# The second copy of K's high and low parts: computed twice, or moved by a DMA inside SBUF

## The chip, the cores and the metric

The kernel runs on one core of one Trainium2 chip. The metric is the device time of one execution in microseconds. A core has TensorE (PE, matrix products, with its weight loads listed apart as PEld), VectorE (DVE), ScalarE (ACT), GpSimd (POOL) and SyncE (SP, which here only issues DMAs), and 16 DMA engines that all queues share.

## The reference

One layer of a decoder trunk on x of 2048 x 1024 floats (one batch entry):

```python
u = x * (1.0 + scale[:, None, :]) + shift[:, None, :]
h = u @ w_in[l]
q, k, v, a_gate, p_in, p_gate, m_a, m_p = jnp.split(h, offsets, axis=-1)
a = sliding_window_sink_attention(q, k, v, sinks[l], bias, mask) * jax.nn.silu(a_gate)
a = a @ w_attn_proj[l]
...                       # a causal pooling branch p, with its own gate and projection
y = jax.nn.sigmoid(m_a) * a + jax.nn.sigmoid(m_p) * p
y = (y @ w_out[l]) * (1.0 + gate[:, None, :])
x = layer_norm(DEEPNORM_ALPHA * x + y, ln_gain[l], ln_bias[l])
```

Attention has 16 query heads of 64 and 2 key/value heads of 64. It goes block by block over 128 positions, and each block of queries sees its own and the preceding block of keys. `shift`, `scale` and `gate` come from a small product with SiLU(c).

## The kernel before, in words

**Two parts of every number.** TensorE is fed with the type float32r. Each operand is split into a high part, a copy into that type by ScalarE (`copy`), and a low part, the difference of the original and the high part, by VectorE (`low`, whose instruction is line 132 of the profile). A product is made as high x high + high x low + low x high (`mm3`): 12 matmuls for a 512 x 512 piece of contraction.

**Fast products.** The large projections are computed with the two-by-two scheme that needs 7 block products where 8 are usual, with 15 sums (Strassen-Winograd). A `Quad` is a pair of output row blocks by two halves of 512 columns. Its moving operands are eight sets in SBUF (`B11`, `T1`, `T2`, `B21`, `T3`, `B22`, `T4`, `B12`), split ahead of time; its weights are loaded raw into `W` and `A22`, summed by GpSimd (lines 294 to 303) and split into `w_set` (lines 325 and 332). `front` makes the first two products of a quad, `back` the other five, and `ring` walks through groups of two quads, two at a time. Between products it calls `tick`, which runs what is hung there: loads, splits, stores.

**Phases.** The sequence is worked in two halves of 1024 positions (s = 0, 1), each as two column halves of 512 (t = 0, 1). The first phase projects K, V and all gates of half 0; then comes attention of half 0 together with its q and pooling projections; then the same two for half 1; then the output projections and the norm. The last ticks of attention of half 0 already compute the first products of the first two quads of half 1. The first of these two is the K/V quad, and the second a gate quad, so K of half 1 is taken as soon as the phase changes.

**The place of the change.** `kv_quad`'s `consume` calls `take_k(s, t, kp)` when the PSUM tile `kp` holds K for 512 positions: rows 0 to 63 are K of kv head 0, rows 64 to 127 of kv head 1. `kk` is an SBUF tile of 128 partitions x (kv head) x (high, low) x (128 + 1024) positions. Attention needs each kv head on both halves of the partitions, since `qs` holds the high part of a query head on one half and its low part on the other. So `take_k` writes each kv head twice: ScalarE copies the high part to the half where it lies (line 697) and VectorE makes the low part (line 132), and then both do it again with the other half as target. This gives 4 copies and 4 differences a call, and 16 of each in all. Line 691 moves the last 128 columns of the first half to the front of the tile for half 1. Attention reads `kk` in `score_mms` (`lg<-kk,qs` in the profile).

**Behind it in `back`.** In a group whose second pair of weights is already split, `back` does for its first quad: add the saved `u` on VectorE (line 380), copy `p5` on ScalarE (line 381, `p<-mm`), form the next sum (line 383), then `consume` (here `take_k`). For its second quad it copies `u2` first (line 376, `u<-mm`), and then lets the product B21 add into the accumulator that was copied.

**What sets the order.** Instructions called through the wrappers `pe`, `act`, `dve`, `pool` and `sp` (line 56) stay in program order on their engine. Those called through `nc.scalar`, `nc.vector`, `nc.gpsimd` and `nc.sync` are placed by a planner that uses its own costs and due times; it also sets all semaphores. `take_k` uses the second kind. TensorE's order is fixed throughout. An engine's queue is worked strictly in order, SP's too: a DMA that waits for its source or for its room holds up those behind it.

Of the kernel before, what the change touches and what calls it, by code (L numbers as in the profile page):

```python
# [23 lines left out]
CH = 512  # L24
# [3 lines left out]
HD = 64  # L28
# [31 lines left out]
def kernel(  # L60
# [22 lines left out]
    nc = tc.nc  # L83
# [44 lines left out]
    def as32(ap):  # L128
        return ap.bitcast(F32)

    def low(engine, dst, src, hi):
        engine.tensor_tensor(dst, src, as32(hi), ALU.subtract)  # L132
# [416 lines left out]
    def kv_quad(s):  # L549
        vts = []  # L550

        def consume(ph, mi, t, src):
            if mi == 0:
                if s == 0 and t == 0:
                    place_kv(ph)
                take_k(s, t, src)
            else:
                vt = ph.c("vt")
                nc.scalar.copy(vt, src)
                vts.append((t, vt))  # L560

        def turn(i):
            if s > 0 and i == 0:
                nc.vector.tensor_copy(vv[:, 0], vv[:, 2 * NB])
            turn_v(*vts[i])

        return Quad((win[TK], win[TV]), consume), turn
# [121 lines left out]
    def take_k(s, t, kp):  # L689
        if s > 0 and t == 0:  # L690
            nc.vector.tensor_copy(kk[:, :, :, 0:P], kk[:, :, :, 2 * CH :])
        c0 = P + t * CH
        for kv in range(2):
            src = kp[kv * HD : kv * HD + HD, :]
            for half in (kv, 1 - kv):
                dst = kk[half * HD : half * HD + HD, kv, :, c0 : c0 + CH]
                nc.scalar.copy(dst[:, 0, :], src)
                low(nc.vector, dst[:, 1, :], src, kk[kv * HD : kv * HD + HD, kv, 0, c0 : c0 + CH])

    def bias_rows():  # L700
        room = cp.tile([P, 4 * D], F32, tag="set_T2", name="head_T2")
# [683 lines left out]
    kk = vv = None  # L1385
# [127 lines left out]
```

## Time and profile before

| | |
|---|---|
| median of 3 runs | 1752.56 us (1752.3 to 1756.21) |
| profiled execution, span from the first to the last instruction | 1751.3 us |
| granted TensorE clock, mean | 0.993 |
| ScalarE K copies (line 697) | 16, mean 582 ns |
| VectorE K differences (line 132, `kk<-mm,kk`) | 16, mean 688 ns |
| K written, half 0 | 384.8 to 400.9 us |
| K written, half 1 | 689.1 to 709.1 us |
| first scores of attention | 417.7 us |

No time of the profiled execution is known besides its span; it is 1.3 us under the median of the runs. In the profile's rows a group reads: line, engine, operation, output<-input by the program's names, shapes, count. A row of the timeline begins with the start and the duration in us and may end with how long the engine had stood idle and which instruction ended that. The rows of a table by stretches give the length of the stretch, the busy time of the engines (with counts), TensorE's granted clock, the DMA engines' share and their GB/s.

### The profile page before, as it was taken

How to read it: one execution, taken by the hardware profiler on the slowest of the kernel's cores; microseconds unless marked ns; L12 is line 12 of the kernel's file. 1: busy time of each engine (PE TensorE's matmuls, PEld its weight loads, DVE VectorE, ACT ScalarE, POOL GpSimd, SP SyncE). 2: the span in 40 equal slices, each digit the busy share in tenths (PEclk: the TensorE clock that was granted, in tenths of full speed). 3: DMA queues.
4: the chain of work that ended last, by engine and by line, in shares of the span. 5: the costliest groups of instructions: out<-in, count | busy, mean ns of one | idle time of the engine just before them, and what ended most of it. 6: DMA issues, size and time to landing. Idle time of an engine off the chain costs nothing.

```text
span 1751.3 us, 24998 instructions
## 1 busy us (share of the span) xinstructions
PE 1697.7 (97%) x8248; PEld 1427.4 (82%) x8248; DVE 1205.2 (69%) x2178; ACT 934.0 (53%) x1973; POOL 798.3 (46%) x618
## 2 busy tenths in 40 slices
PE   6899999999999998999999999999999999999996
PEld 5688888878888887888788888888888878887785
DVE  5977665655777777767645357777768696865777
ACT  4644444545777776545444367777745353423452
POOL 2154444441356567434424124555773572463542
PEclk9999999999999999999999999999999999999999
DMA  9384758743354558687777634544698675699432
GB/s 365 117 283 177 276 204 280 257 155 132 114 169 142 178 187 318 237 284 255 276 265 257 234 111 133 180 140 157 232 351 289 185 265 194 216 341 360 157 139 102
DMA packets 185843, 381.31 MB, mean 218 GB/s; under 512 B 18785, under 2 KB 39281, under 8 KB 185713
## 3 DMA queue, kind: packets, MB, share of 16 engines
q1 hardware_dynamic: 179072, 363.92, 59.7%
q0 software_dynamic: 3552, 11.56, 1.7%
q10 hardware_dynamic: 3088, 4.23, 0.8%
q8 instruction: 65, 1.06, 0.2%
q14 instruction: 66, 0.53, 0.1%
HBM read 244.35 MB, written 138.44 MB: 219 GB/s over the span
## 4 chain that ended last, share of the span: by engine, by line
PE 42%; POOL 3%; DVE 2%; DMA 2%; issue 1%; ACT 1%; POOLq 0%; SPq 0%; DVEq 0%; ACTq 0%
PE mm L56 25%; PE lg L56 14%; PE pv L56 2%; PE pt L56 1%; DMA set_T<-ain_T_split 1%; DVE w_set L132 1%; POOL nxt L56 1%; POOL W L298 0%; DVE wide L56 0%; POOL p L56 0%; POOL wide L601 0%; DMA W<-in_wap_dram 0%; POOL rs L56 0%; ACT L L56 0%; POOL a L56 0%
## 5 line engine op out<-in xcount | busy, mean ns | idle before, releaser
L56 PE MATMUL mm<-set_B,w_set 128*128 128x512 f32 x3240 | 799.0, 395 | 12.6 <-ACT u L376 6.3
L56 PEld LDWEIGHTS mm<-set_B,w_set 128*128 128x128 f32 x3240 | 603.2, 189 | 140.7 <-DVE w_set L132 8.8
L56 PE MATMUL lg<-set_T,w_set 128*128 128x512 f32 x2088 | 504.4, 392 | 11.8 <-DVE w_set L132 5.1
L56 PEld LDWEIGHTS lg<-set_T,w_set 128*128 128x128 f32 x2088 | 391.3, 188 | 99.5 <-DVE w_set L132 8.0
L132 DVE TENSOR_TENSOR w_set<-W,w_set 128x1024 fp32r<-128x1024 f32 x162 | 224.0, 1383 | 182.7 <-ACT w_set L325 172.1
L325 ACT CAST w_set<-W 128x1024 fp32r<-128x1024 f32 x162 | 170.6, 1053 | 291.1 <-PE mm L56 221.6
L56 PE MATMUL mm<-set_T,w_set 128*128 128x512 f32 x1080 | 265.6, 394 | 0.0
L56 PEld LDWEIGHTS mm<-set_T,w_set 128*128 128x128 f32 x1080 | 200.7, 188 | 41.1
L294 POOL TENSOR_TENSOR W<-W,A 128x512 f32<-128x512 f32 x56 | 83.8, 1497 | 218.3 <-DMA W<-in_win_dram 59.4
L303 POOL TENSOR_TENSOR W<-W 128x512 f32<-128x512 f32 x56 | 83.5, 1492 | 165.5 <-DVE w_set L132 150.3
L56 DVE TENSOR_TENSOR o<-pv,o 64x128 f32<-64x128 f32 x256 | 72.4, 283 | 88.6 <-ACT o L56 85.5
L56 ACT ACTIVATE L<-L,nm 128x257 f32<-128x257 f32 (+1 forms) x256 | 127.7, 501 | 9.4 <-DVE nm L56 3.9
L298 POOL TENSOR_TENSOR W<-W 128x512 f32<-128x512 f32 x56 | 90.9, 1624 | 78.6 <-DVE w_set L132 68.9
L56 DVE CUSTOM_DVE_ANT_0 L<-lg,bt,nsink 128x256 f32<-128x256 f32 (+1 forms) x256 | 111.6, 473 | 5.0 <-PE lg L56 0.8
L299 POOL TENSOR_TENSOR W<-W 128x512 f32<-128x512 f32 x56 | 88.6, 1582 | 33.6 <-DMA W<-in_win_dram 26.6
L56 POOL TENSOR_TENSOR w_set<-W,w_set 128x1024 fp32r<-128x1024 f32 x14 | 33.7, 2410 | 139.7 <-ACT w_set L56 97.0
L56 POOL TENSOR_TENSOR p<-nxt,pg 128x512 f32<-128x512 f32 x32 | 41.9, 1311 | 107.0 <-DVE sm L56 104.6
L56 ACT COPY o<-pv 64x256 f32<-64x256 f32 x128 | 47.5, 371 | 76.7 <-PE pv L56 76.0
L56 DVE TENSOR_TENSOR ptl<-pt,pth 128x512 fp32r<-128x512 f32 (+1 forms) x128 | 85.8, 670 | 1.9 <-ACT pth L56 1.7
L56 PE MATMUL lg<-kk,qs 128*128 128x256 f32 (+1 forms) x512 | 80.5, 279 | 0.0
L56 ACT ACTIVATE L<-L,sm 128x256 f32<-128x256 f32 (+1 forms) x128 | 64.5, 504 | 30.0 <-DVE sm L56 30.0
L56 DVE TENSOR_TENSOR k_lo<-spare,k_hi 128x512 fp32r<-128x512 f32 x61 | 60.4, 992 | 28.5 <-ACT k_hi L56 13.4
(216 smaller groups left out, 2308.2 us busy)
## 6 DMA issues: line engine op xcount, KB each, us to landing
W<-in_win_dram SPq DMA_DIRECT2D x48, 512.0 KB, 5.2
w_set<-wmix_d SPq DMA_DIRECT2D x32, 512.0 KB, 5.2
W<-in_win_dram SPq DMA_DIRECT2D x34, 256.0 KB, 3.2
A<-in_win_dram SPq DMA_DIRECT2D x34, 256.0 KB, 5.0
ag_d<-sig SPq DMA_DIRECT2D x32, 256.0 KB, 3.9
pg_d<-sig SPq DMA_DIRECT2D x32, 256.0 KB, 3.8
ma_d<-sig SPq DMA_DIRECT2D x32, 256.0 KB, 3.9
mp_d<-sig SPq DMA_DIRECT2D x32, 256.0 KB, 3.8
```

Source lines behind the costliest of these rows:

```text
L56: return lambda *args, **kw: self.tc.keep_in_program_order(op(*args, **kw))
L132: engine.tensor_tensor(dst, src, as32(hi), ALU.subtract)
L294: e.tensor_tensor(self.w[:, 1, :], self.w[:, 2, :], self.a22, ALU.add)
L298: e.tensor_tensor(x[:, 1, :], x[:, 1, :], x[:, 0, :], ALU.subtract)
L299: e.tensor_tensor(x[:, 2, :], x[:, 0, :], x[:, 2, :], ALU.subtract)
L303: e.tensor_tensor(x[:, 3, :], x[:, 3, :], x[:, 1, :], ALU.subtract)
L325: a.copy(by_two(hi), raw)
```

## The change

For each kv head `take_k` now makes the high and the low part once, on the half of the partitions where K lies. Both are then brought to the other half by one DMA from SBUF to SBUF (64 partitions x 2 x 512 floats, 256 KB), issued by `nc.sync` and placed by the planner. There are two such transfers a call and 8 in the kernel, in place of 8 copies and 8 differences.

```diff
@@ def take_k(s, t, kp)
         for kv in range(2):
             src = kp[kv * HD : kv * HD + HD, :]
-            for half in (kv, 1 - kv):
-                dst = kk[half * HD : half * HD + HD, kv, :, c0 : c0 + CH]
-                nc.scalar.copy(dst[:, 0, :], src)
-                low(nc.vector, dst[:, 1, :], src, kk[kv * HD : kv * HD + HD, kv, 0, c0 : c0 + CH])
+            dst = kk[kv * HD : kv * HD + HD, kv, :, c0 : c0 + CH]
+            nc.scalar.copy(dst[:, 0, :], src)
+            low(nc.vector, dst[:, 1, :], src, dst[:, 0, :])
+            nc.sync.dma_start(as32(kk[(1 - kv) * HD : (2 - kv) * HD, kv, :, c0 : c0 + CH]), as32(dst))
```

## The prediction

> **What bounds the kernel now.** First the page's head, then the list of who waited for whom on the TensorE, then the busy time of three stretches: the end of the first projection phase and the start of attention (372 to 421 us), the stretch in which the second K tile is first written (689 to 696 us), and the rest of the second projection phase.
>
> ```profile
> span 1751.3 us, 24998 instructions
> PE 1697.7 (97%) x8248; PEld 1427.4 (82%) x8248; DVE 1205.2 (69%) x2178; ACT 934.0 (53%) x1973; POOL 798.3 (46%) x618
> PE mm L56 <- ACT u L376: 6.3, 1, 6.3
> 372.00:421.00 49.00, 49.00 (x223) 40.42 (x222) 25.68 (x37) 23.00 (x36) 6.14 (x4) 1.00 0.34 113
> 689.00:696.00 7.00, 0.70 (x3) 0.39 (x2) 4.98 (x9) 3.51 (x7) 5.31 (x5) 0.73 1.02 411
> 696.00:1011.00 315.00, 313.53 (x1380) 258.84 (x1380) 184.60 (x202) 146.59 (x225) 115.55 (x80) 1.00 0.74 260
> ```
>
> TensorE is busy 97% of the span, so work taken from ScalarE or VectorE counts only where TensorE stands still for it. Around the first phase's K writes it does not: 49.00 of 49.00 us are busy. Before the second phase's first K write it does, once, for 6.3 us, and the engine that it waits for is ScalarE, with the copy `u` of line 376. In that stretch the DMA engines are full (share 1.02, 411 GB/s). The timeline of all engines there:
>
> ```profile
> 686.38 1.39 SPq L56 DMA_DIRECT2D set_T<-u_T_split  x3
> 686.40 2.91 PE L56 MATMUL lg<-set_T,w_set 128*128 128x512 f32 x12
> 689.13 0.58 ACT L697 CAST kk<-mm 64x512 fp32r<-64x512 f32 x1
> 690.49 0.68 DVE L132 TENSOR_TENSOR kk<-mm,kk 64x512 fp32r<-64x512 f32 x1
> 690.54 1.26 POOL L56 TENSOR_TENSOR a<-o,ag 128x512 f32<-128x512 f32 x1 [1.66 <-DVE o L56]
> 691.20 0.58 ACT L697 CAST kk<-mm 64x512 fp32r<-64x512 f32 x1 [1.49 <-DVE kk L132]
> 691.82 0.69 DVE L132 TENSOR_TENSOR kk<-mm,kk 64x512 fp32r<-64x512 f32 x1 [0.65 <-ACT kk L697]
> 692.53 0.58 ACT L697 CAST kk<-mm 64x512 fp32r<-64x512 f32 x1 [0.75 <-DVE kk L132]
> 693.88 0.58 ACT L697 CAST kk<-mm 64x512 fp32r<-64x512 f32 x1 [0.76 <-DVE kk L132]
> 694.48 0.59 ACT L381 COPY p<-mm 128x512 f32<-128x512 f32 x1
> 694.97 0.59 ACT L376 COPY u<-mm 128x512 f32<-128x512 f32 x1
> 695.61 10.03 PE L56 MATMUL mm<-set_B,w_set 128*128 128x512 f32 x36 [6.30 <-ACT u L376]
> ```
>
> Four K copies stand on ScalarE ahead of the copies `p` and `u`, and from the second on each waits for the VectorE difference before it. Even the third, which reads the other 64 rows of the same PSUM tile, does so. Copy and difference alternate at about 1.35 us a pair. `u` saves an accumulator that the B21 product then adds into, so TensorE stops from 689.3 to 695.6.
>
> **Part by part.** The K instructions and their users, from the answer on the tile `kk`:
>
> ```profile
> L56 PE MATMUL lg<-kk,qs x512: 220/281/288, 417.7 to 1276.7; 128*128 128x256 f32 x160, 128*128 128x128 f32 x11
> L697 ACT CAST kk<-mm x16: 573/582/586, 384.8 to 707.8; 64x512 fp32r<-64x512 f32 x16
> L132 DVE TENSOR_TENSOR kk<-mm,kk x16: 674/688/695, 386.1 to 708.4; 64x512 fp32r<-64x512 f32 x16
> L691 DVE CAST kk<-kk x1: 428/428/428, 400.9 to 400.9; 128x512 fp32r<-128x512 f32 x1
> busy tenths in 40 slices 0000000013444443100000034444400000000000
> 400.18 0.69 DVE L132 TENSOR_TENSOR kk<-mm,kk 64x512 fp32r<-64x512 f32 x1 [0.65 <-ACT kk L697]
> 413.02 0.76 DVE L132 TENSOR_TENSOR vv<-pt,vv 128x256 fp32r<-128x256 f32 x2 [9.26 <-ACT vv L685]
> ```
>
> *Removed:* 8 ScalarE copies of 0.582 us and 8 VectorE differences of 0.688 us, 4.7 and 5.5 us of engine time. In the first phase that is worth nothing, since TensorE has no gap there to close. In the second, the two pairs at 692.53 and 693.88 go. `p` also has a floor: it fills a tile of the new phase where attention's buffers lay, and the POOL product that read the last of these ends at 690.54 + 1.26 = 691.80. The second copy ends at 691.78, so the floor does not bite. `u` moves from 694.97 to about 692.3 and TensorE restarts near 692.95: **2.65 us** earlier.
>
> *Added:* 8 transfers of 256 KB (64 rows of 2 x 512 floats) on SP's queue, 2 per K write. Their landing is covered in both phases. The first scores of attention start at 417.7, 17.5 us after the last difference at 400.18. In the second phase the line of tenths shows `kk` unused from slice 17 to 22, hundreds of microseconds. The copy of line 691 now has to wait on VectorE for the last two transfers. Behind it are weights and V of the first phase, but VectorE is idle 9.26 us before 413.02, so I cost it at nothing (without that cover, about one landing). On SP the first phase's transfers stand ahead of attention's first weights and the gate stores; TensorE's gapless 49 us say that these come early, so nothing again, and one issue each if they did not.
>
> *What is late next.* SP's queue does not move with TensorE in this place:
>
> ```profile
> SPq L56 <- DMA ain_T<-a: 12.6, 1, 12.6
> ain_T<-a POOLq DMA_DIRECT2D x2, 256.0 KB, 4.7
> ain_B<-a SPq DMA_DIRECT2D x1, 256.0 KB, 2.0
> 703.02 0.34 SPq L56 DMA_DIRECT2D A<-in_win_dram  x1
> 704.02 0.59 SPq L56 DMA_DIRECT2D set_T<-u_T_split  x1
> set_T<-u_T_split SPq DMA_DIRECT2D x1, 1024.0 KB, 7.9
> 705.48 8.32 PE L56 MATMUL lg<-set_T,w_set 128*128 128x512 f32 x36
> 720.24 1.67 DVE L132 TENSOR_TENSOR w_set<-W,w_set 128x1024 fp32r<-128x1024 f32 x1 [0.57 <-ACT w_set L325]
> 722.73 2.88 PE L56 MATMUL mm<-set_B,w_set 128*128 128x512 f32 x12
> ```
>
> SP stands 12.6 us, until 703.02, because room for the next weights is freed by POOL's four stores of attention's last tiles. Those hang on POOL and the DMA engines, not on TensorE. Only then come the weights `A`, `W` and the second half of set T4 at 704.02, which lands 7.9 us later, at 711.9. TensorE needs that half after two T3 products and half of a T4 product, 30 of the 36 matmuls from 705.48: 705.48 + 30 x 8.32/36 = 712.4. The slack is **0.5 us**. A second check is the next pair's weights: the VectorE difference ends at 721.91, TensorE takes it with the third matmul from 722.73, at about 723.2, slack 1.3 us. So of the 2.65 us about 0.5 is kept and the rest is spent waiting for T4.
>
> *What the new transfers cost there.* The first pair is ready at 691.2 and 692.5, when the DMA engines are full: 0.52 MB at 411 GB/s is 1.3 us of their time, ahead of POOL's stores. SP's restart, and with it T4, slips by 0 to 1.3; I take 0.6, the middle, as stores of another queue share the engines with it. The second pair comes when SP issues T4 and the next weights. Two issues of 0.34 to 0.59 us each and again up to 1.3 us of traffic give 0 to 2 us, against slack that is partly there; I take 0.3 on the path. **Sum: -0.5 + 0.6 + 0.3 = +0.4 us**; its ends are -0.5 and 1.3 + 2 - 0.5 = +2.8.
>
> The SBUF page of the Trainium skill ("SBUF — State Buffer", Door 1: The DMA port swizzle) speaks against the change: 64 partitions reach half of the DMA ports and get about half the rate. By it each pair would weigh 2.6 us rather than 1.3 and the sum would be about +1.4 us; no K transfer is in this trace to show it.
>
> *The clock.* The stall also costs TensorE speed. The rows give the length of a stretch, TensorE's busy time in it and the granted clock; the stretches are cut where the clock steps. The last row is a wait in the last phase:
>
> ```profile
> 67.53:70.95 3.42, 2.39 (x6) 0.50 0.90 319
> 1624.01:1627.42 3.41, 1.63 (x7) 1.00 0.72 222
> 688.76:692.17 3.41, 0.55 (x3) 1.00 1.03 406
> 692.17:695.59 3.42, 0.00 (x0) 0.50 1.03 422
> 695.59:699.00 3.41, 3.39 (x8) 0.50 1.03 407
> 1626.77 4.12 PE L56 MATMUL mm<-set_B,w_set 128*128 128x512 f32 x10 [1.78 <-DVE w_set L132]
> ```
>
> A stretch of 3.41 us with little work is followed by half clock, and a full one lifts it again. The 36 matmuls at 695.61 took 10.03 us, those at 705.48 only 8.32: 1.7 us lost. With the shorter stall, 692.17 to 695.59 would hold about 2.6 us of work. The nearest row, 2.39 us, did not lift the clock, so I expect half clock until 699.0 and no gain from it. TensorE then reaches T4 only 1.3 us early (692.95 to 699.0 at half rate does 3.0 us' worth instead of 1.7). If 2.6 us does lift it, TensorE reaches T4 3.0 us early. Either way it waits there, so the sum stands. The Trainium skill ("TensorE: Matmul & The Clock Gate", Part 1) drops the clock after an idle window of about 3.4 us; this trace differs, for it drops already after one with 1.63 us of work. A wait at T4 of 1.8 us or more could thus cost up to 1.7 us again.
>
> Everything behind runs on TensorE's order and moves with it. The instructions without a fixed order are placed by the planner with its own costs, so some may change place. A wait of TensorE for a weight difference that came late took 1.78 us (at 1626.77), so I allow 2 us either way for one such. Profiled time +0.4 on a span of 1751.3; the median of the runs is 1752.56, 1.3 us above the span: **1752.9 us**.
>
> **Rivals.**
> *Faster: the gain is kept.* T4's half is not late, because the planner issues it elsewhere or POOL's stores land sooner. Then 2.65 to 3.0 us are kept: 1749.6 to 1749.9. If the planner also puts `u` ahead of the K copies, TensorE restarts about 0.6 us after 689.7, 5.3 us early, and the half-clock stretch shrinks by up to 1.7: 1745.6. For it: the chain is exactly what the change cuts. Against it: SP's 12.6 us, with 0.5 us of slack.
> *Slower: SP waits for K.* SP works in order. If the planner puts the first pair ahead of the three fills of 686.38, these wait for the second difference, 691.82 + 0.69 = 692.5, 6.1 us later. POOL's stores then come behind fills that are still landing, and T4's half slips by up to as much, to 718.0, 5.6 us after 712.4; the long wait costs up to 1.7 us of clock: +7.3, 1759.9. Half of the slip, without the clock, gives +2.6, 1755.2, and so about does a second pair that stands ahead of T4's half. For it: that queue is already the late one. Against it: the fills are ready before the differences. It decides from a slip of 0.5 us on.
> *It doesn't shorten the chain.* Should the second copy wait for the first transfer (a store of 256 KB from SP landed in 2.0 us here, the row of `ain_B` above), `u` comes no earlier; then it is the transfers' cost alone, +0.9 to +3, about 1754.5.
>
> **Numbers.** Forecast, mostly handed back, 0.50, own range 1750 to 1756; gain kept 0.18; SP late 0.24; no shortening 0.08. A measurement of this kernel can tell about 0.3% from no change, 5.3 us. Over 5.3 us faster: 0.10 of the second case and 0.02 from the planner. Over 5.3 us slower: 0.15 of the third, 0.04 of the fourth, 0.07 from the planner. That is 0.12, 0.62 and 0.26. The range runs from between the two ends of the kept gain, 1747.5, to nearly the full price of a late SP, 1759.5.
>
> **What would show it.** 8 copies of line 697 instead of 16; the wait of TensorE for `u` near 3.7 us; T4's half landing at or after 712 and TensorE waiting about 1 us for it; SP still stopped by `ain_T` until 703 to 704. I am wrong if that wait for T4 is absent, if SP stands before 690 on a K difference, or if the phase ends over 3 us from its old place in either direction.

## The result, and the profile after

| | before | after |
|---|---|---|
| median | 1752.43 us (1749.67 to 1756.21) | 1763.16 us (1761.81 to 1764.2) |
| profiled execution: time, span | span 1751.3 us | 1764.2 us, span 1762.4 us |
| granted TensorE clock, mean | 0.993 | 0.990 |

The ratio after to before is 1.0056, 95% interval [1.0043, 1.0068] (it is not the quotient of the two medians, which is 1.0061): about 10 us slower, and outside the range of the prediction. The first lines are the head of the profile of after, and from its lists of waits two rows of TensorE and two of SP's queue (what waited, for whom, us in total, times, longest):

```profile
span 1762.4 us, 24998 instructions
PE 1703.5 (97%) x8248; PEld 1431.1 (81%) x8248; DVE 1200.0 (68%) x2170; ACT 926.9 (53%) x1965; POOL 797.9 (45%) x618
PE lg L56 <- DMA set_T<-u_T_split: 7.7, 2, 5.0
PE mm L56 <- ACT u L376: 3.6, 1, 3.6
SPq L56 <- DMA ain_T<-a: 10.3, 1, 10.3
SPq L698 <- DVE kk L132: 8.2, 5, 4.9
```

The work taken away is gone: 8 instructions less on ScalarE and on VectorE, 7.1 and 5.2 us less busy time (more than eight copies on ScalarE, because its other copies were a few ns shorter in this execution). TensorE's wait for the copy `u` fell from 6.3 to 3.6 us, as forecast. But a wait that was not there before, 7.7 us for the fills of T3 and T4 (`set_T<-u_T_split`), has taken its place. The last row gives the agent away: SP's queue stood 8.2 us, in five places, waiting for K differences of VectorE, 5.6 us of it in two places between 686 and 712 us.

The tile `kk` in after, and the stretches that the prediction cut (busy time of PE, PEld, DVE, ACT, POOL, then clock, DMA share, GB/s):

```profile
L696 ACT CAST kk<-mm x8: 576/580/582, 385.0 to 701.6; 64x512 fp32r<-64x512 f32 x8
L698 SPq DMA_DIRECT2D kk<-kk x8: 590/610/661, 386.9 to 709.0; - x8
L691 DVE CAST kk<-kk x1: 417/417/417, 403.4 to 403.4; 128x512 fp32r<-128x512 f32 x1
DMA to landing us min/median/max: 3.0/3.7/8.0
```
```profile
372.00:421.00 49.00, 49.00 (x222) 40.41 (x221) 22.61 (x33) 20.63 (x31) 6.34 (x4) 1.00 0.43 136
689.00:696.00 7.00, 3.37 (x11) 2.53 (x11) 4.70 (x8) 2.82 (x5) 5.43 (x5) 0.86 0.49 145
696.00:1011.00 315.00, 303.49 (x1309) 248.91 (x1308) 181.53 (x196) 140.46 (x216) 115.07 (x80) 0.98 0.75 260
```

The first half of the sequence is untouched (TensorE 49.00 of 49.00 us again). In 689 to 696 TensorE does 3.37 us of work instead of 0.70, yet the DMA engines fell from a share of 1.02 to 0.49: there was nothing for them to do, because the fills had not been issued. The stretch behind pays: 303.49 instead of 313.53 us busy. The timeline of after at this place:

```profile
685.67 0.42 SPq L758 DMA_DIRECT2D ag<-ag_d  x1
691.08 2.01 SPq L698 DMA_DIRECT2D kk<-kk  x2
691.70 0.69 DVE L132 TENSOR_TENSOR kk<-mm,kk 64x512 fp32r<-64x512 f32 x1 [0.65 <-ACT kk L696]
691.71 0.58 ACT L381 COPY p<-mm 128x512 f32<-128x512 f32 x1
692.84 10.07 PE L56 MATMUL mm<-set_B,w_set 128*128 128x512 f32 x36 [3.63 <-ACT u L376]
693.18 2.45 SPq L56 DMA_DIRECT2D set_T<-u_T_split  x3
706.98 7.38 PE L56 MATMUL lg<-set_T,w_set 128*128 128x512 f32 x24 [2.71 <-DMA set_T<-u_T_split]
707.17 0.35 SPq L56 DMA_DIRECT2D A<-in_win_dram  x1
708.26 1.29 SPq L698 DMA_DIRECT2D kk<-kk  x2
709.60 0.96 SPq L56 DMA_DIRECT2D set_T<-u_T_split  x1
719.36 2.93 PE L56 MATMUL lg<-set_T,w_set 128*128 128x512 f32 x6 [4.99 <-DMA set_T<-u_T_split]
722.79 3.93 PE L56 MATMUL lg<-set_T,w_set 128*128 128x512 f32 x12
726.55 2.88 PE L56 MATMUL mm<-set_B,w_set 128*128 128x512 f32 x12
```

The planner put the first pair of K transfers ahead of the three fills. They wait for the last difference (691.70 + 0.69), and the fills come at 693.18 where they came at 686.38. POOL's stores of attention, which are issued at 696.23 in before and at 696.15 in after, now share the engines with fills that are still landing. The transfers that were in flight in 685 to 700, with KB each and the median time to landing, first in before and then in after:

```profile
set_T<-u_T_split SPq DMA_DIRECT2D x3, 1024.0 KB, 7.4
ain_T<-a POOLq DMA_DIRECT2D x3, 256.0 KB, 3.8
```
```profile
set_T<-u_T_split SPq DMA_DIRECT2D x3, 1024.0 KB, 13.2
ain_T<-a POOLq DMA_DIRECT2D x3, 256.0 KB, 9.0
kk<-kk SPq DMA_DIRECT2D x2, 256.0 KB, 4.7
```

and T4's second half in after, in 700 to 725:

```profile
set_T<-u_T_split SPq DMA_DIRECT2D x1, 1024.0 KB, 9.7
```

SP's stop for `ain_T` therefore ends at 707.17 instead of 703.02. Then the second pair of K transfers stands ahead of T4's second half, which is issued at 709.60 instead of 704.02: 5.6 us late. In after it needed 9.7 us to land (709.60 + 9.7 = 719.3), 7.9 in before. So TensorE, which took it at 712.4, takes it at 719.36, 7.0 us later: 5.6, and 1.8 of slower landing, less the slack of 0.5. The clock also drops with each of the two waits, to 0.50 from 707.8 to 711.1 and again from 718.0 to 724.6. Of the second stretch this is TensorE's row (length, busy time, clock, DMA share, GB/s):

```profile
718.00:724.60 6.60, 5.25 (x14) 0.50 1.05 398
```

The 6 matmuls behind the second wait take 2.93 us (1.39 at the rate of the row at 705.48 in before), the next 12 take 3.93 (2.99 before). The product whose row is below for before is the one at 726.55 in after, 9.7 us late.

```profile
716.83 2.89 PE L56 MATMUL mm<-set_B,w_set 128*128 128x512 f32 x12
```

Later in this execution TensorE loses more: what stands at 848.03 in before is 11.6 us late, and from 872 to 1291 it is 14.1 us, after two waits for weights of 1.81 us (at 859.60) and 0.52 us (at 860.85), the second followed by half clock. The weights come late because the copy of line 325 stands behind two copies `k_hi` on ScalarE, which wait 3.30 and 1.40 us for DMAs there (1.89 and 0.66 us for such in before); why those are late wasn't followed. By 1716 the lag is 11.8 us: 1.6 us of what comes back is clock, since the same wait of 1.78 us in the last phase halved the clock in the profiled execution of before and not in that of after (last section).

### The profile page after: what moved, and what is told of

It is laid out like the page before. It is cut to its first block, busy times and chain, and to the rows that moved or that the text cites. A ratio compares the mean times of both kernels' runs of the same rounds, so it can differ in the third digit from the quotient of the medians.

```text
span 1762.4 us, 24998 instructions
## 1 busy us (share of the span) xinstructions
PE 1703.5 (97%) x8248; PEld 1431.1 (81%) x8248; DVE 1200.0 (68%) x2170; ACT 926.9 (53%) x1965; POOL 797.9 (45%) x618
## 5 line engine op out<-in xcount | busy, mean ns | idle before, releaser
L56 PE MATMUL lg<-set_T,w_set 128*128 128x512 f32 x2088 | 510.3, 395 | 20.7 <-DMA set_T<-u_T_split 7.7
L56 ACT CAST pth<-pt 128x512 fp32r<-128x512 f32 (+1 forms) x128 | 73.4, 573 | 10.4
```

Of the source, the lines that this page charges most:

```text
L56: return lambda *args, **kw: self.tc.keep_in_program_order(op(*args, **kw))
```

## The experiments

All ratios are to the kernel before, run on the same chip, with 95% intervals. "Lag" is read from the profiled execution: how much later than in before the product starts that stands at 716.83 there, less the same difference at the product that stands at 686.40, since executions arrive at this place up to 1.8 us earlier or later. After has a lag of 9.72 + 0.10 = +9.8 us. A lag belongs to one execution: that of "first pair late" was 5.2 us faster than the median of its ten runs, the others lie within 3.6 us of theirs.

**Theory A:** the place of the K transfers on SP's queue, ahead of the fills and of T4's second half, costs the time. **Rivals:** their bytes do, wherever they stand; the shorter chain itself moved something; the first half of the sequence has a part in it.

| kernel | median us | ratio | lag us |
|---|---|---|---|
| both pairs late | 1750.4 | 0.9984 [0.9969, 0.9998] | -0.6 |
| both pairs late, again | 1752.07 | 0.9988 [0.9979, 0.9996] | -1.4 |
| half 1's transfers small, in place | 1759.21 | 1.0028 [1.0017, 1.0040] | +6.8 |
| change in half 1 only | 1761.14 | 1.0038 [1.0024, 1.0051] | +9.2 |
| change in half 0 only | 1752.66 | 1.0000 [0.9991, 1.0009] | +0.4 |
| before, plus the transfers | 1762.5 | 1.0045 [1.0029, 1.0060] | +10.1 |
| first pair late | 1756.75 | 1.0014 [1.0003, 1.0024] | +1.7 |
| second pair late | 1757.34 | 1.0023 [1.0012, 1.0034] | +3.5 |
| both late, T4's half earlier | 1751.46 | 0.9988 [0.9979, 0.9997] | -2.6 |
| early `u`, without the change | 1757.73 | 1.0019 [1.0009, 1.0028] | -0.5 |
| early `u` and T4's half earlier, without the change | 1761.85 | 1.0048 [1.0034, 1.0062] | -0.7 |

The expectations in us were set against 1752.43 us for before. In the rounds of the experiments before had medians of 1754.66 us (first run of both late, small transfers, half 1 only, added transfers), 1753.63 (half 0 only, one pair late, T4's half earlier) and 1753.71 (second run of both late, early `u`), so ratios are compared and not medians. Turned into times on 1752.43 us, three ratios lie under what theory A expected: small transfers (1757.3 against 1759 to 1764), half 1 only (1759.1 against 1761 to 1765, inside the range of its rival), and the added transfers (1760.3 against 1763 to 1767; there the median of 1762.5 lies under it too).

**Both pairs late.** The transfers are hung eight ticks later in the fixed order, so that they stand behind T4's second half.

```diff
-            nc.sync.dma_start(as32(kk[(1 - kv) * HD : (2 - kv) * HD, kv, :, c0 : c0 + CH]), as32(dst))
+            other = kk[(1 - kv) * HD : (2 - kv) * HD, kv, :, c0 : c0 + CH]
+            defer(8, lambda other=other, dst=dst: sp.dma_start(as32(other), as32(dst)))
```

> The changed kernel with its K transfers hung 8 ticks later and kept in program order on SP, so that they stand behind the fills of sets T3 and T4 and behind the next weights. Theory A (SP's order: the fills wait behind the K transfers, which wait for the K differences): the fills are issued at 686 to 688 again, TensorE's two waits for set_T vanish, TensorE restarts near 692.9 and the time falls back to 1750 to 1755. Theory B (the bytes: 0.5 MB of half-partition transfers in a full DMA system): the same bytes now meet the next weights, 1756 to 1762. Theory C (the planner has put other instructions elsewhere, as in the second delay near 858 us): 1758 to 1763.

> The kernel with the change, its K transfers hung eight ticks later, once more with more rounds, to settle whether it is under the kernel before. Theory A (the shorter stall is worth about 0.5 us in place, the transfers nothing when they stay behind the fills): 1750 to 1753, ratio 0.998 to 1.000. Rival (the first ratio of 0.9984 was the scatter of the phase's start between executions): ratio 1.000 to 1.001.

The timeline of the second of the two runs:

```profile
686.12 1.40 SPq L56 DMA_DIRECT2D set_T<-u_T_split  x3
692.70 10.10 PE L56 MATMUL mm<-set_B,w_set 128*128 128x512 f32 x36 [3.64 <-ACT u L376]
703.04 0.59 SPq L56 DMA_DIRECT2D set_T<-u_T_split  x1
710.51 1.66 PE L56 MATMUL lg<-set_T,w_set 128*128 128x512 f32 x6 [0.92 <-DMA set_T<-u_T_split]
712.49 1.31 SPq L56 DMA_DIRECT2D kk<-kk  x2
```

With the fills back at 686 and T4's half at 703 the loss is gone, and the kernel is 0.12% to 0.16% under before in two comparisons. The same 256 KB transfers and the same halved K work, only at another place on SP's queue, are worth the whole difference. The shorter stall is seen in both runs (3.64 us), and of its 2.65 us TensorE hands back 0.92 here and 1.78 in the first run while it waits for T4's second half. The lags say that 1.4 and 0.6 us are kept in place; the forecast was 0.5.

**Half 1's transfers small.** The transfers keep their places and their waits, but in half 1 they carry 16 of 512 columns; the rest of that move is left out.

```diff
+            n = CH if s == 0 else 16
+            other = kk[(1 - kv) * HD : (2 - kv) * HD, kv, :, c0 : c0 + n]
+            nc.sync.dma_start(as32(other), as32(dst[:, :, 0:n]))
```

> The changed kernel, but in the second half of the sequence each K transfer carries 16 columns instead of 512; the rest of the other partitions keeps the first half's K, so this leaves out part of the move. The place in SP's queue and the wait for the difference stay, 97% of the bytes go. Theory A: still slow, 1759 to 1764, with the fills at 692 to 693. Theory B: 1751 to 1754. Theory C: no clear forecast, near the changed kernel.

```profile
693.08 1.78 SPq L56 DMA_DIRECT2D set_T<-u_T_split  x3
710.12 0.59 SPq L56 DMA_DIRECT2D set_T<-u_T_split  x1
715.93 2.93 PE L56 MATMUL lg<-set_T,w_set 128*128 128x512 f32 x6 [4.37 <-DMA set_T<-u_T_split]
```

Fills and T4's half are as late as in after (693.18 and 709.60 there), with 97% of the bytes gone. What the bytes add is the landing: the half is taken at 715.93 instead of 719.36. By the lag, order alone makes 6.8 of 9.8 us; by the ratios, half (1.0028 of 1.0056, with intervals of 1.0017 to 1.0040 and 1.0043 to 1.0068). The waiting is thus about half of it or more, the bytes the rest, and the rest comes only on top of the wrong place, since late transfers with all their bytes cost nothing.

**Change in one half only.** K is made as before for s = 0, or for s = 1.

```diff
+            if s == 0:          # in the other kernel: s == 1
+                for half in (kv, 1 - kv):
+                    ...
+                continue
```

> The change made only for the second half of the sequence; the first half computes K twice as before. Theory A: the whole loss, 1761 to 1765, since TensorE had no gap in the first half. Theory C, if part of the loss comes from what moved in the first half: 1754 to 1760.

> The change made only for the first half of the sequence; the second half computes K twice as before. As predicted for that half: no gap of TensorE to close and the landing covered, so as before, within 1752 to 1756, with the 6.3 us wait for u back. If the first half's transfers cost something of their own (weights of attention held up on SP), 2 us or more above the kernel before.

What can be measured lies in half 1. In half 0 neither the 4 copies and 4 differences saved nor the 4 transfers are worth anything measurable, as forecast. Half 1 alone gives 1.0038; its interval overlaps that of after, so that the 1.0056 of the whole isn't shown to need the first half, nor shown to be free of it. At the start of the phase its lag is nearly that of after, 9.2 of 9.8 us. Behind it, between 725 and 872 us of before, the execution of after loses 4.4 us more and this one 0.2, the loss of which the cause stays open.

**Before, plus the transfers.** K is made twice as before, and the 8 transfers are added.

```diff
             for half in (kv, 1 - kv):
                 ...
+            own = kk[kv * HD : kv * HD + HD, kv, :, c0 : c0 + CH]
+            nc.sync.dma_start(as32(kk[(1 - kv) * HD : (2 - kv) * HD, kv, :, c0 : c0 + CH]), as32(own))
```

> The kernel before, with nothing saved and the 8 K transfers added at the end of each kv head's work (they rewrite the same values). Theory A: the transfers again stand ahead of the fills, and the last difference ends 1.4 us later than in the changed kernel, so 1763 to 1767. Theory B: the bytes alone, 1753 to 1757. If the saved copies mattered as I predicted, this is at least 2.65 us slower than the changed kernel.

```profile
695.24 10.87 PE L56 MATMUL mm<-set_B,w_set 128*128 128x512 f32 x36 [6.29 <-ACT u L376]
695.60 2.82 SPq L56 DMA_DIRECT2D set_T<-u_T_split  x3
719.79 2.93 PE L56 MATMUL lg<-set_T,w_set 128*128 128x512 f32 x6 [5.47 <-DMA set_T<-u_T_split]
```

Here TensorE waits the full 6.29 us for `u` and still takes T4's half at 719.79, within 0.5 us of after. Its ratio and after's overlap. So the 2.65 us that the shorter chain saves don't show in the time of after: they are spent waiting for T4.

**One pair late.** Only the pair of t = 0, or only that of t = 1, is hung eight ticks later; the other stays with the planner.

```diff
+            if t == 0:          # in the other kernel: t == 1
+                defer(8, lambda other=other, dst=dst: sp.dma_start(as32(other), as32(dst)))
+            else:
+                nc.sync.dma_start(as32(other), as32(dst))
```

> The changed kernel with only the first pair of K transfers (t = 0) moved 8 ticks later; the second pair keeps its place ahead of the second fill of T4. If the order of the first pair is what costs (the three fills late by 6.8 us, POOL's stores behind them, SP's restart 4 us late), the fills are back at 686 to 688, SP restarts near 703, and only the second pair's 1.3 us of issue and its bytes stand before T4's half: 1750 to 1754. If each pair costs alike, 1755 to 1758.

> The changed kernel with only the second pair of K transfers (t = 1) moved 8 ticks later; the first pair stays ahead of the three fills. If the first pair's order is what costs: the fills at 693, SP's restart near 707, T4's half issued 1.3 us earlier than in the changed kernel: 1757 to 1761. If each pair costs alike, 1754 to 1757.

First the kernel whose first pair is late, then the one whose second pair is late:

```profile
685.94 1.39 SPq L56 DMA_DIRECT2D set_T<-u_T_split  x3
703.04 1.36 SPq L702 DMA_DIRECT2D kk<-kk  x2
704.45 0.73 SPq L56 DMA_DIRECT2D set_T<-u_T_split  x1
713.45 1.65 PE L56 MATMUL lg<-set_T,w_set 128*128 128x512 f32 x6 [2.95 <-DMA set_T<-u_T_split]
```
```profile
694.67 8.45 PE L56 MATMUL mm<-set_B,w_set 128*128 128x512 f32 x36 [3.63 <-ACT u L376]
695.01 2.37 SPq L56 DMA_DIRECT2D set_T<-u_T_split  x3
709.53 0.60 SPq L56 DMA_DIRECT2D set_T<-u_T_split  x1
717.34 1.66 PE L56 MATMUL lg<-set_T,w_set 128*128 128x512 f32 x6 [1.32 <-DMA set_T<-u_T_split]
```

Each pair does its own part. The second pair alone in place, ahead of T4's half, gives 1.0014, which is 0.0026 to 0.0030 above both late, about 5 us. The first pair alone in place, ahead of the fills, gives 1.0023, 0.0035 to 0.0039 above both late, 6 to 7 us. Together that is 11 to 12 us, and after stands 0.0068 to 0.0072, 12 to 13 us, above both late. Such differences carry 2 to 3 us of doubt each, so the sum is right within them. The lags of the single executions add up less well: 2.7 and 4.5 us above the mean of both late, -1.0, against 10.8 for both pairs in place. Of the missing 3.6 us, 2.5 are clock behind T4's half: from taking it to the product by which the lag is read, after needs 7.19 us, because its wait of 4.99 us is followed by half clock, and these two kernels need 4.69 and 4.70, with full clock (1.00) behind waits of 2.95 and 1.32 us. The first of the two profiled executions is also the one that was 5.2 us under its median, so 2.7 us may be too little for the second pair.

**T4's half still earlier.** Both pairs late, and T4's second half issued directly behind its first, ahead of the weights that wait for POOL's stores.

```diff
-        for p, name, half in ((0, "T3", 0), (1, "T3", 1), (3, "T4", 0), (5, "T4", 1)):
+        for p, name, half in ((0, "T3", 0), (1, "T3", 1), (3, "T4", 0), (4, "T4", 1)):
```

> The late transfers of all four K writes, and the second fill of set T4 hung one tick earlier, so that it stands on SP ahead of the load that waits for POOL's stores. With late transfers alone TensorE still waited 1.8 us for that fill. If that fill was what took the rest of the 2.65 us back, this wait goes and the time is 1 to 2 us under the late transfers alone: 1748 to 1751. If its 1 MB, now ahead of POOL's stores in a full DMA system, delays SP's restart by up to 2.5 us, the next weights come late instead and there is no gain, 1750 to 1754.

1751.46 us, ratio 0.9988 [0.9979, 0.9997]. The wait for T4 is gone from the list of waits, and in place the whole shorter stall is kept, a lag of -2.6 us. SP starts again only at 707.31, 2.5 us later than the shift of this execution explains (703.02 + 1.8), with a fourth fill of 1 MB ahead of POOL's stores. By the ratios nothing is gained over both pairs late (0.9984 and 0.9988). In the profiled execution 0.4 us go at the product of 721.95, whose 12 matmuls took 3.28 us (2.88 before), and 1.6 us in the last phase, where the clock dropped in this execution and in neither of both late (last section).

**No stall at all.** Not the change, but its aim pushed to the end: on the kernel before, the second quad's `u` and its product B21 are done in attention's last ticks; in a second kernel T4's half is also moved as above.

```diff
-            elif n == 65:
-                product(opened[0][0], pair(0, 1)[0], "B21")
+            elif n in (65, 67):
+                product(opened[n // 67][0], pair(n // 67, 1)[0], "B21")
...
-            if n == 64:
-                opened[0].append(nxt_group[0].w[:, 0, :])
-                act.copy(opened[0][4], opened[0][0])
+            if n in (64, 66):
+                x = (n - 64) // 2
+                opened[x].append(nxt_group[x].w[:, 0, :])
+                act.copy(opened[x][4], opened[x][0])
```

> Kernel before, K made twice as before; only the second quad's copy u and its B21 product are moved into the last ticks of attention, so that TensorE has no K copy to wait for at the start of half 1's first phase. Theory A (SP's queue, stopped until POOL's stores have freed room, sets the place of this phase, through the second half of T4): the 6.3 us stall and the half clock behind it go, TensorE is 6 to 8 us ahead at the phase's start, but then waits for T4's second half at about 712, so that by 720 at most 1 us is left: 1751 to 1754, ratio 0.999 to 1.001. Rival B (the stall itself was the cost, and what is late next is late only because the stall let it be): 4 us or more are kept, 1746 to 1749, ratio 0.996 to 0.998.

> As the kernel with the early u, and in addition the second half of T4 is loaded one tick earlier, directly behind the first half, ahead of the weights that wait for POOL's stores. Theory A: the wait for T4 goes, and the next on SP's late queue is the next pair's weights, which had 1.3 us of slack in the kernel before and are also behind POOL's stores; the fill, now ahead of these, delays them by up to 4 us as in the kernel that had the late K transfers and this edit. TensorE waits for the weights' difference near 722 instead: 1750 to 1753, ratio 0.998 to 1.000. Rival B (only T4's second half held it): 5 us or more are kept, 1745 to 1748, ratio 0.995 to 0.997.

```profile
690.99 3.06 PE L56 MATMUL mm<-set_B,w_set 128*128 128x512 f32 x12 [0.45 <-ACT W L56]
698.37 7.36 PE L56 MATMUL mm<-set_B,w_set 128*128 128x512 f32 x24 [4.32 <-DVE mm L383]
705.57 6.96 PE L56 MATMUL lg<-set_T,w_set 128*128 128x512 f32 x30
712.84 1.66 PE L56 MATMUL lg<-set_T,w_set 128*128 128x512 f32 x6 [0.32 <-DMA set_T<-u_T_split]
```

Both theories missed the times. In the rows of the first, TensorE restarts 4.6 us before 695.61 and is back at its old place by 705.57. That is what A said, but T4 isn't the agent (0.32 us): TensorE stops 4.32 us for the sum of line 383, whose operand `p` is copied behind the K chain. The time is lost elsewhere, because the edit also acts at the start of the output phase. There the trace shows a second such wait, of 3.84 us at 1298.70, and TensorE goes from 1.4 us behind before (at 1291) to 6.7 (at 1298). In the second kernel SP is stopped until 707.35, and TensorE is 4.8 us behind by 725.45. These two kernels show that the K chain holds more than one step of the phase; they don't test the change itself.

## Why the prediction was wrong, point by point

- *The saved K work shortens the chain to `u` by 2.65 us, TensorE restarts near 692.95.* Right: 692.84, a wait of 3.63. The floor, POOL's read at 691.80, also held: `p` starts at 691.71. The rival in which the second copy waits for a transfer, and the one in which the planner puts `u` ahead, didn't happen.
- *Half 0 is worth nothing.* Right: 1.0000 [0.9991, 1.0009].
- *The copy of line 691 waits for the transfers and costs nothing.* Right: 403.4 instead of 400.9, TensorE busy throughout.
- *Half clock until 699.0 behind the shorter stall, so that TensorE is only 1.3 us early at T4.* Mis-sized, without consequence. In after the clock was at half from 694.1 to 697.5 only, the 36 matmuls took 10.07 us (10.03 before), and the next product started 2.7 us early (702.75 for 705.48). With the first pair late it came nearly as forecast: half clock until 698.4, 11.18 us, and 1.5 us early after the shift of that execution. TensorE waits for the fills behind it either way. The stretches that the prediction took from before lie at another place in each execution, as the last section shows.
- *The gain is mostly handed back at T4's second half.* Right in kind, shown with both pairs late, where the waits for it were 0.92 and 1.78 us; 1.4 and 0.6 us stayed by the lags (2.1 and 2.8 us by the ratios), where 0.5 was forecast. In after itself nothing of it stayed.
- *The K transfers come when the DMA engines are full, and cost 1.3 us of their time ahead of POOL's stores.* **This step failed.** It took from the times at which the sources are ready, 691.2 and 692.5, that the pair would stand behind the fills of 686.38. On a queue that works strictly in order a place isn't a time. The planner puts an `nc.sync` transfer where its own costs say; it stood ahead, and what was charged as 0.6 us of traffic was 6.8 us of a standing queue. The argument against that rival, "the fills are ready before the differences", is an argument about the chip, not about the planner that had already decided.
- *The second pair, 0.3 us on the path.* Mis-sized by the same step: ahead of T4's half it cost about 5 us by the medians and 2.7 by the lags, as two transfers of 256 KB were issued before, and landed with, the half that TensorE needs next.
- *The rival "SP waits for K", +2.6 to +7.3 us with a chance of 0.24.* Its mechanism is what happened; its price was too low. The slip of the fills was 6.8 us (6.1 forecast), and to it came the second pair ahead of T4 (which the rival named as another way to +2.6, not as an addition), slower landing by 1.8 us, and a clock that fell at two waits. The later loss, from 9.7 to 14.1 us around 850 of before, no step had. In the experiments with the K transfers the same stretch loses between 0.2 and 1.3 us, 1.3 with the change in half 0 only; whether every execution of after has the 4.4 isn't shown, and what sets it stays open.
- *The port rule, by which 64 partitions reach half of the DMA ports* ("SBUF — State Buffer", Door 1: The DMA port swizzle, of the Trainium skill). The K transfers took 3.0 us at the least and 3.7 in the median, where a store of 256 KB landed in 2.0 us in before. That goes the way of the rule, but other transfers were in flight beside them, and no run here isolated the ports.

What the profile of after was to show against the forecast was named rightly: SP stood on a K difference before 690 (after the issue at 685.67 its next is the K transfer at 691.08), and the phase ended more than 3 us from its old place.

## What to carry to other kernels

A DMA that replaces compute is also an entry in an in-order queue: ask where the planner will put it and which loads will stand behind its wait, before its bytes are counted. Where a queue feeds the critical path, hang the new transfer at a fixed place behind the loads that are due first; here that turned 1.0056 into 0.9988 with the same instructions. And put a price on a standing queue twice: once for the wait, once for what the late transfers then share the DMA engines with.

## What the runs showed of the hardware

The same stall doesn't cost the same clock. After a wait for `u` of 3.62 to 3.65 us the same 36 matmuls took 10.06 to 10.10 us in after and with both pairs late, 10.97 with small transfers, 11.18 with the first pair late, and 8.45 with the second pair late. The busy time of the engines and then the clock in 693.80 to 695.50, first with small transfers, then with the second pair late:

```profile
693.80:695.50 1.70, 1.70 (x5) 1.32 (x4) 0.70 (x1) 0.48 (x1) 1.70 (x2) 0.50 0.63 159
```
```profile
693.80:695.50 1.70, 0.83 (x4) 0.70 (x5) 1.67 (x3) 0.82 (x2) 1.62 (x2) 1.00 0.74 157
```

In the second kernel the stall lay between 691.04 and 694.67 and the clock stayed at 1.00. In the first it lay between 689.12 and 692.77, and the clock was at half from about 691.3 to 698.2, two of the 3.41 us stretches of the prediction; in after it was one, from about 694.1 to 697.5. How the stall falls on those stretches fits this, but no run was made for it.

A wait that the change doesn't touch shows the same. In the last phase TensorE stops 1.77 or 1.78 us for a weight difference in every kernel. Behind it the 10 matmuls took 4.12 us in before (the prediction's row at 1626.77), 4.16 with both late and T4's half earlier, 4.14 and 3.77 in the two kernels with early `u`, and 2.55 to 2.60 in the nine other profiled executions, after among them:

```profile
1640.66 2.58 PE L56 MATMUL mm<-set_B,w_set 128*128 128x512 f32 x10 [1.78 <-DVE w_set L132]
```

So one profiled execution can be 1.2 to 1.6 us slower than another behind one and the same wait.

The stores of another queue feel a late fill: the same three POOL stores of 256 KB, issued at 696.2 us, landed after 3.8 us when the fills had been issued at 686.4, and after 9.0 us when they came at 693.2. The bytes of the K transfers aren't the reason: with small transfers, and fills at 693.08, the stores took 9.6 us, and with the first pair late, and fills at 685.94, 4.9 us.
